# The down product of an encoder MLP: operands split one step earlier, table work one product earlier, tail scalings reordered

## The chip, the cores and the metric

One core of a Trainium2 chip runs the whole program. The metric is the device time of one execution in microseconds (us); of several runs the median is taken. Lower is better.

## The reference

Two residual layers on a sequence of 1024 tokens with 1024 channels, all in float32. Layer 0 mixes tokens by multi-scale pooling, layer 1 by differential attention with rotary tables. After each mixer comes the same MLP, and the last layer is followed by one RMSNorm:

```python
h = h + mixer(rms_norm(h, mix_norm[i]))
h = h + conv_ffn(rms_norm(h, ffn_norm[i]), ...)     # both layers
return rms_norm(h, final_norm)                      # y * rsqrt(mean(y*y) + eps) * final_norm

def conv_ffn(x, w_up, conv_w, conv_b, w_down):      # D_FF = 2816
    g, u = split(x @ w_up)
    return (gelu(conv3(g) + conv_b) * u) @ w_down   # the last product is the "down" product
```

The attention of layer 1 needs cos and sin of positions times inverse frequencies (the rotary tables) and a number lambda from four 64-element vectors.

## The kernel before, in words

The program runs in stages: pooling, up stage and down stage of layer 0, attention, up stage and down stage of layer 1. The change lies in the two down stages (function `ffn`, lines 546 to 708) and in the work handed to them: `attention_tables` (885) for layer 0, `final_gain` (1368) and `tail1` (1373) for layer 1.

**Exact products from a fast format.** Each float32 operand is split into a rounded part and a rest: ScalarE copies it into the rounded format (`hi`, line 580), VectorE subtracts (`lo`, line 581). Each product is then three matmuls (hi by hi, hi by lo, lo by hi, line 597).

**The down stage.** A seven-product Strassen scheme is used. The products run in the order `DOWN_ORDER = (1, 2, 6, 7, 4, 5, 3)`. Each has six chunks of the contraction: the first, c = 0, is one block of 256 rows of the weights, the other five are two. A pair of product and chunk is called a step here: steps 0 to 41, six to a product, so that product 1 is steps 0 to 5 and product 3, the last, steps 36 to 41. In every step TensorE goes over four column tiles t = 0 to 3 of the left operand; a step with c = 0 has 12 matmuls, any other 24. Four PSUM banks, one for each t, collect a product. Products 1, 6 and 5 start in fresh banks; the others add on what is there. After a product's last chunk `evict` (609) takes bank t: VectorE adds it to half a row tile of the result (616) and, after the products that finish a half, ScalarE squares that half and sums it (607), for the norm that follows. Product 1's banks are copied by ScalarE (612). Product 2 finishes the first half of tiles 4 to 7, product 4 the first half of tiles 0 to 3, product 5 their second half, product 3 the second half of tiles 4 to 7.

**Operands.** `load_down(s)` (555) loads both operands of step s by two DMAs of up to 512 KB from SyncE's queue (SP), `prep_down(s)` (570) splits them: four instructions, hi and lo of the left operand `m`, hi and lo of the weights `w`; when it ends it issues `load_down(s + 3)`. The split operands lie in the four half-buffers of `hnT` by turns, in steps 36 to 39 in two of them alone (layer 0 fills the other two with the transposed result of tiles 0 to 3 at that time), and in steps 40 and 41 in two buffers `dop` of their own.

**The order is written by hand.** In the down stage the instructions of TensorE, VectorE, ScalarE and SP keep the order in which the code issues them (726). After the matmuls of each t, and after the eviction where there is one, `pump` (651) is called once. It takes the next piece of the first waiting `prep_down`, if that is for a step no more than two ahead of the running one (one ahead for steps 36 to 39), and otherwise a piece of the list `work`. A piece that ends a `prep_down` also lets `pump` go on with the next. `work` gets the last products of the up stage, `add_p1` (622) after product 2, and after product 4 what `extra` gives: the rotary tables and lambda in layer 0, the load of the final norm's weight in layer 1. After product 5 `tails` (628) puts the norm and scaling of tiles 0 to 3 between the matmuls of product 3. In layer 0 that is `norm_to_hnT` (202): ScalarE scales a tile (`xs`, 204), TensorE transposes it (212), the copies are split into `hnT` (131, 132). In layer 1 it is `tail1`: VectorE scales each half by the row's factor and the norm's weight (1377), SP stores it (1378).

**The end of the stage.** Steps 40 and 41 are run together for one t after the other. After each t come its eviction, the row factor `rstd` (180: add, ScalarE's square root, four more small VectorE instructions) and at once the scaling of that tile. In layer 0 the transposes of a tile follow two tiles later.

**Around it.** Outside these stretches a scheduler places the instructions; in the attention stage only TensorE's order is written out. Weights of the attention are loaded and split in gaps of layer 0's down stage.

Of the kernel before, what the change touches and what calls it, by code (L numbers as in the profile page):

```python
# [20 lines left out]
P = 128  # L21
# [68 lines left out]
def trunk_kernel(  # L90
# [47 lines left out]
    def row_bcast(ap):  # L138
        return ap.partition_broadcast(P)
# [223 lines left out]
    def ffn(layer, ar, tail, extra=None):  # L363
# [205 lines left out]

        def prep_down(s):  # L570
            n = CHUNKS[steps[s][1]][1]
            k = s % 4 if s < last else 2 + s % 2
            if s < len(steps) - 2:
                hi, lo = (t[:, 4 * (k % 2):4 * (k % 2) + 4] for t in hnT[k // 2])
            else:
                hi, lo = ar.dop[s % 2]
            ops = []
            for x, o in zip(stage.pop(s), (0, 2)):
                h_, l_ = hi[:, o:o + n], lo[:, o:o + n]
                A.copy(h_, x)  # L580
                V.tensor_tensor(l_, x, f32(h_), ALU.subtract)  # L581
                ops += [h_, l_]
                yield
            dops[s] = ops
            if s > 1:
                load_down(s + 3)
# [60 lines left out]
        def down_all():  # L647
# [2 lines left out]

            def pump(k=1):
                for _ in range(k):
                    if queue and queue[0][0] <= now[0] + (1 if last <= queue[0][0] < len(steps) - 2 else 2):
                        if next(queue[0][1], "end") == "end":
                            queue.pop(0)
                            pump()
                    elif work:
                        if next(work[0], "end") == "end":
                            work.pop(0)
# [8 lines left out]
            for s, (i, c) in enumerate(steps[:-2]):  # L668
                now[0] = s
                while s not in dops:  # L670
                    pump()
                if s < NT:
                    tt = (s + 4) % NT
                    nc.sync.dma_start(ar.h[tt], h_dram[3 * layer][tt])
                fresh = i in (1, 6, 5) and c == 0
                for t in range(4):
                    if fresh:
                        banks[t] = ar.tile("ps_up", [P, 512], F32, "dn")
                    mms(s, t, fresh, c == nc_ - 1)
                    if c == nc_ - 1:  # L680
                        evict(i, t)
                    pump()
                    next(after, None)
                if c == nc_ - 1:
                    if i == 2:
                        work.append(add_p1())
                    elif i == 4 and extra is not None:
                        work.append(extra())
                    elif i == 5:
                        after = tails()  # L690
# [5 lines left out]
            for t in range(4):  # L696
                for s in (len(steps) - 2, len(steps) - 1):
                    mms(s, t, False, s == len(steps) - 1)
                evict(3, t)
                tl = tail(t + 4, rstd(sq[1][:, t:t + 1]))  # L700
                next(tl, None)
                ends.append(tl)
                if t > 1:
                    for _ in ends[t - 2]:
                        pass
            for tl in ends[2:]:
                for _ in tl:
                    pass

        load(0)  # L710
        first = prep(0)
# [12 lines left out]
                load(j + 2)  # L724
        ar.open_down()
        with tc.manual_schedule(engines=ENGINES | {mybir.EngineType.SP}):
            down_all()


    xr = x.rearrange("b (t p) d -> (b t) p d", p=P)  # L730
# [154 lines left out]
    def attention_tables():  # L885
# [7 lines left out]
        posi = w[:, 816:816 + NT].bitcast(positions.dtype)  # L893
        nc.sync.dma_start(inv, cst[:, C_INV:C_INV + 32])
        nc.sync.dma_start(posi, positions.rearrange("(t p) -> p t", p=P), allow_slow_non_contiguous=True)
        V.tensor_copy(posf, posi)
        yield
        for t in range(NT):
# [18 lines left out]
        A.activation(sinT, nn, AF.Sin)  # L917
        A.activation(cosT, nh, AF.Sin)
        yield
        l = ar.tile("gc", [P, D], F32, "lam")  # L920
        lv = l[:, 0:256].rearrange("p (i f) -> p i f", f=64)
        lp = l[:, 256:384].rearrange("p (i f) -> p i f", f=64)
        ls, le = l[:, 384:386], l[:, 386:388]
        for i, src in enumerate((lam_q1, lam_k1, lam_q2, lam_k2)):
            nc.sync.dma_start(lv[:, i], row_bcast(src[0]))
        V.tensor_tensor(lp, lv[:, 0:4:2], lv[:, 1:4:2], ALU.mult)
        V.tensor_reduce(ls, lp, AX.X, ALU.add)
        A.activation(le, ls, AF.Exp)
        V.tensor_tensor(neglam, le[:, 1:2], le[:, 0:1], ALU.subtract)
        V.tensor_scalar(neglam, neglam, -LAM_INIT, None, ALU.add)  # L930
        nc.sync.dma_start(subsc, subln[0].rearrange("(e o) -> e o", o=1))
        V.tensor_scalar(subsc, subsc, 1.0 - LAM_INIT, None, ALU.mult)


# [433 lines left out]
    def final_gain():  # L1368
        fin.append(ar.tile("gc", [P, D], F32, "gf"))
        nc.sync.dma_start(fin[0], row_bcast(final_norm))  # L1370
        yield

    def tail1(tt, r):
        y, gf = ar.h[tt], fin[0]
        for n in range(2):
            hs = halves(y)[n]
            V.scalar_tensor_tensor(hs, hs, r, halves(gf)[n], ALU.mult, ALU.mult)
            nc.sync.dma_start(halves(outr[tt])[n], hs)
            if n == 0 and tt < 4:
                yield  # L1380
        return
        yield

    for _ in mlp:
# [28 lines left out]
```

## Time and profile before

| | |
|---|---|
| median of 3 runs | 2119.53 us (2117.35 to 2125.2) |
| the profiled execution, its own time | 2117.11 us |
| its span, first to last instruction | 2115.3 us |
| TensorE matmul busy | 2015.5 us, 95% of the span |
| VectorE / ScalarE / GpSimd busy | 1558.6 / 1020.1 / 899.8 us |
| mean granted TensorE clock | 0.98 of full speed |
| down stage of layer 0, of layer 1 | 528 to 760 us, 1886 to 2115.3 us |

Times of rows are microseconds from the start of the span; durations in the timeline are us. PE is TensorE, PEld its weight load, DVE VectorE, ACT ScalarE, POOL GpSimd, SP SyncE. A busy PE is not PE at its peak, since its matmuls are pipelined: the distance from one matmul's start to the next says more than the busy share. In the timeline a bracket gives the idle time of the engine just before the instruction and what ended it. PEclk is the granted TensorE clock as a share of full speed.

### The profile page before, as it was taken

Reading aid. Unit: us, or ns where it says so; the run is one execution under the profiler, and the core shown is the slowest. Engines: PE = TensorE matmul, PEld = TensorE weight load, DVE = VectorE, ACT = ScalarE, POOL = GpSimd, SP = SyncE. Lnnn points to the kernel's source line nnn. Section 1 sums busy time; section 2 is a strip of 40 time slices with the busy share of each in tenths; the row PEclk is TensorE's granted clock in tenths of the full one; section 3 lists DMA queues with packets and bytes.
Section 4 is the critical chain, followed back from the end, with each engine's and each line's share of the span. In section 5 each row is a group of like instructions: output and inputs, shape, how many; then the busy total and the mean of one; then the engine's idle time right before and its main releaser. Section 6 shows DMA issues by size and latency. Waiting matters only on the chain.

```text
span 2115.3 us, 27608 instructions
## 1 busy us (share of the span) xinstructions
PE 2015.5 (95%) x9659; PEld 1669.5 (79%) x9659; DVE 1558.6 (74%) x2278; ACT 1020.1 (48%) x1830; POOL 899.8 (43%) x689
## 2 busy tenths in 40 slices
PE   6789999999999799999999998987999999999997
PEld 5678888888888677888888887876888888888885
DVE  7867777777584648899889987767667777774646
ACT  7643333333453545676667666555433333344433
POOL 4599999995000000101110111024999999920000
PEclk8899999999999999999999999998999999999999
DMA  4225454554965412122212216253346445467653
GB/s 168 95 84 181 138 190 138 158 177 144 375 211 174 163 54 67 48 72 62 61 46 73 57 40 224 90 189 110 120 144 198 146 161 167 139 227 278 205 201 130
DMA packets 221720, 301.90 MB, mean 143 GB/s; under 512 B 17852, under 2 KB 142092, under 8 KB 218764
## 3 DMA queue, kind: packets, MB, share of 16 engines
q1 hardware_dynamic: 221580, 300.13, 43.4%
q8 instruction: 76, 1.25, 0.2%
q14 instruction: 64, 0.52, 0.1%
HBM read 196.78 MB, written 90.70 MB: 136 GB/s over the span
## 4 chain that ended last, share of the span: by engine, by line
PE 82%; DVE 9%; ACT 3%; DMA 3%; issue 2%; SPq 1%; POOL 0%; DVEq 0%; ACTq 0%; POOLq 0%
PE dn L597 17%; PE up_b L422 16%; PE up_c L422 11%; PE up_a L422 11%; PE pj L1020 6%; PE sc L1106 4%; PE pj L1062 4%; PE po L1148 3%; PE aT L1137 2%; PE pj L1233 2%; DVE nm L1108 1%; PE pp L844 1%; PE pl L824 1%; ACT hnT_hi L580 1%; DVE hnT_lo L581 1%
## 5 line engine op out<-in xcount | busy, mean ns | idle before, releaser
L1088 POOL TENSOR_TENSOR q_lo<-qt,q_hi 128x256 fp32r<-128x256 f32 x64 | 49.7, 777 | 698.3 <-ACT q_hi L1087 616.8
L380 POOL TENSOR_TENSOR w_lo<-s,w_hi 128x512 fp32r<-128x512 f32 x168 | 274.2, 1632 | 17.7 <-ACT w_hi L379 17.2
L597 PE MATMUL dn<-hnT_hi 128*128 128x512 f32 x584 | 229.7, 393 | 12.0 <-ACT hnT_hi L580 11.8
L597 PE MATMUL dn<-hnT_lo,hnT_hi 128*128 128x512 f32 x584 | 230.2, 394 | 4.4 <-DVE hnT_lo L581 4.4
L597 PE MATMUL dn<-hnT_hi,hnT_lo 128*128 128x512 f32 x584 | 228.8, 392 | 0.0
L422 PE MATMUL up_b<-x_hi,w_hi 128*128 128x512 f32 x528 | 207.2, 392 | 5.3 <-ACT x_hi L304 4.4
L422 PE MATMUL up_b<-x_lo,w_hi 128*128 128x512 f32 x528 | 206.6, 391 | 2.3 <-DVE x_lo L305 2.3
L380 POOL TENSOR_TENSOR w_lo<-raw,w_hi 128x512 fp32r<-128x512 f32 x130 | 195.3, 1503 | 30.6 <-ACT w_hi L379 26.4
L422 PE MATMUL up_b<-x_hi,w_lo 128*128 128x512 f32 x528 | 206.2, 391 | 0.0
L379 ACT CAST w_hi<-s 128x512 fp32r<-128x512 f32 x176 | 108.4, 616 | 178.9 <-PE up_b L422 87.4
L1108 DVE TENSOR_REDUCE nm<-sc 128x1 f32<-128x1024 f32 x128 | 155.7, 1216 | 15.4 <-PE sc L1106 14.6
L1111 ACT ACTIVATE prob<-sc,nm 128x1024 f32<-128x1024 f32 x128 | 142.7, 1115 | 22.3 <-DVE nm L1108 11.7
L422 PE MATMUL up_a<-hnT_hi,w_hi 128*128 128x512 f32 x352 | 139.3, 396 | 1.4 <-ACT g L499 0.9
L597 PEld LDWEIGHTS dn<-hnT_hi 128*128 128x128 f32 x584 | 110.5, 189 | 37.1 <-ACT hnT_hi L580 13.5
L422 PE MATMUL up_a<-hnT_lo,w_hi 128*128 128x512 f32 x352 | 138.9, 395 | 0.1
L422 PE MATMUL up_a<-hnT_hi,w_lo 128*128 128x512 f32 x352 | 138.5, 394 | 0.0
L394 POOL TENSOR_TENSOR s<-raw 128x512 f32<-128x512 f32 x84 | 133.1, 1584 | 10.3 <-DMA raw<-in_ffn_w_up_dram 4.1
L422 PE MATMUL up_c<-hnT_hi,w_lo 128*128 128x512 f32 x352 | 137.0, 389 | 0.2 <-DVE w_lo L380 0.2
L422 PE MATMUL up_c<-hnT_hi,w_hi 128*128 128x512 f32 x352 | 136.9, 389 | 0.0
L422 PE MATMUL up_c<-hnT_lo,w_hi 128*128 128x512 f32 x352 | 136.9, 389 | 0.0
L581 DVE TENSOR_TENSOR hnT_lo<-mst,hnT_hi 128x1024 fp32r<-128x1024 f32 (+1 forms) x80 | 90.2, 1127 | 61.3 <-ACT hnT_hi L580 61.1
L597 PEld LDWEIGHTS dn<-hnT_lo,hnT_hi 128*128 128x128 f32 x584 | 110.5, 189 | 31.0 <-DVE hnT_lo L581 8.4
(298 smaller groups left out, 5362.6 us busy)
## 6 DMA issues: line engine op xcount, KB each, us to landing
raw<-in_ffn_w_up_dram SPq DMA_DIRECT2D x88, 512.0 KB, 4.3
mst<-m_dram SPq DMA_DIRECT2D x70, 512.0 KB, 5.8
wd<-in_ffn_w_down_dram SPq DMA_DIRECT2D x22, 1024.0 KB, 6.0
wd_dram<-wd SPq DMA_DIRECT2D x22, 1024.0 KB, 6.4
m_dram<-cm SPq DMA_DIRECT2D x80, 256.0 KB, 5.6
wst<-wd_dram SPq DMA_DIRECT2D x40, 512.0 KB, 4.8
m_dram<-gc SPq DMA_DIRECT2D x66, 256.0 KB, 6.3
wst<-in_ffn_w_down_dram SPq DMA_DIRECT2D x30, 512.0 KB, 6.1
```

What stands on the lines that cost most here:

```text
L379: A.copy(hi, src)
L380: eng.tensor_tensor(lo, src, f32(hi), ALU.subtract)
L394: eng.tensor_tensor(t, a, b, op)
L422: PE.matmul(acc, l[a][:, k], r[b][:, k], start=first and n == 0, stop=n == 11, skip_group_check=True)
L581: V.tensor_tensor(l_, x, f32(h_), ALU.subtract)
L597: PE.matmul(banks[t], l[:, q, cols], r[:, q], start=first and cnt == 0, stop=stop and cnt == 3 * n - 1, skip_group_check=True)
L1020: PE.matmul(acc, l[:, k % 2, h], r[:, k], start=(n == 0), stop=(n == 3 * NK - 1))
L1062: PE.matmul(acc, l[:, k % 4], r[:, k], start=(n == 0), stop=(n == 3 * NK - 1))
L1106: PE.matmul(sc[:, ns_], l[:, c], ks[:, c, ns_], start=(l is qhi), stop=(l is qlo))
L1108: V.tensor_reduce(nm, sc, AX.X, ALU.max, negate=True)
L1111: A.activation(soft[j, i][c], sc, AF.Exp, bias=nm, accum_out=sm[:, c, i:i + 1])
L1148: PE.matmul(po, l[:, k], r[:, k], start=(n == 0), stop=(n == 3 * NT - 1))
```

## The change

Nothing of what is computed changes, and the number of matmuls stays. In `ffn`:

```diff
         def prep_down(s):
             n = CHUNKS[steps[s][1]][1]
-            k = s % 4 if s < last else 2 + s % 2
-            if s < len(steps) - 2:
-                hi, lo = (t[:, 4 * (k % 2):4 * (k % 2) + 4] for t in hnT[k // 2])
+            if s < last or s in (last + 2, last + 3):
+                hi, lo = (t[:, 4 * (s % 2):4 * (s % 2) + 4] for t in hnT[s % 4 // 2])
             else:
                 hi, lo = ar.dop[s % 2]
...
-                    if queue and queue[0][0] <= now[0] + (1 if last <= queue[0][0] < len(steps) - 2 else 2):
+                    if queue and queue[0][0] <= now[0] + 3:
...
-                    elif i == 4 and extra is not None:
+                    elif i == 7 and extra is not None:
                         work.append(extra())
...
                 evict(3, t)
-                tl = tail(t + 4, rstd(sq[1][:, t:t + 1]))
-                next(tl, None)
-                ends.append(tl)
+                if t:
+                    next(ends[t - 1], None)
+                ends.append(tail(t + 4, rstd(sq[1][:, t:t + 1])))
                 if t > 1:
                     for _ in ends[t - 2]:
                         pass
-            for tl in ends[2:]:
-                for _ in tl:
-                    pass
+            next(ends[3], None)
+            return ends[2:]
...
         with tc.manual_schedule(engines=ENGINES | {mybir.EngineType.SP}):
-            down_all()
+            ends = down_all()
+        for tl in ends:
+            for _ in tl:
+                pass
```

Steps 36, 37, 40 and 41 now use the two `dop` buffers, steps 38 and 39 the second `hnT` pair. In the last part the scaling of a tile is issued after the eviction of the next one and ahead of that one's `rstd`; what is left of the last two tiles (in layer 0 their transposes, copies and stores) comes after the stretch with the order written by hand.

In `attention_tables` the loads of the four lambda vectors and of `subsc` are issued with those of the frequencies and positions, and four empty pieces follow before the first instruction that uses them:

```diff
+        for i, src in enumerate((lam_q1, lam_k1, lam_q2, lam_k2)):
+            nc.sync.dma_start(lv[:, i], row_bcast(src[0]))
+        nc.sync.dma_start(subsc, subln[0].rearrange("(e o) -> e o", o=1))
+        for _ in range(4):
+            yield
         V.tensor_copy(posf, posi)
...
-        for i, src in enumerate((lam_q1, lam_k1, lam_q2, lam_k2)):
-            nc.sync.dma_start(lv[:, i], row_bcast(src[0]))
         V.tensor_tensor(lp, lv[:, 0:4:2], lv[:, 1:4:2], ALU.mult)
...
-        nc.sync.dma_start(subsc, subln[0].rearrange("(e o) -> e o", o=1))
```

For layer 1's end, the final norm's weight is multiplied into the finished first halves of tiles 4 to 7 as pieces of `work`; the last scaling of such a half is then ScalarE's, and the second half comes first:

```diff
         nc.sync.dma_start(fin[0], row_bcast(final_norm))
-        yield
+        for _ in range(8):
+            yield
+        for tt in range(4, NT):
+            hs = halves(ar.h[tt])[0]
+            V.tensor_tensor(hs, hs, halves(fin[0])[0], ALU.mult)
+            yield
 
     def tail1(tt, r):
         y, gf = ar.h[tt], fin[0]
-        for n in range(2):
+        for n in (1, 0):
             hs = halves(y)[n]
-            V.scalar_tensor_tensor(hs, hs, r, halves(gf)[n], ALU.mult, ALU.mult)
+            if n == 0 and tt >= 4:
+                A.mul(hs, hs, r)
+            else:
+                V.scalar_tensor_tensor(hs, hs, r, halves(gf)[n], ALU.mult, ALU.mult)
             nc.sync.dma_start(halves(outr[tt])[n], hs)
-            if n == 0 and tt < 4:
+            if n and tt < 4:
                 yield
-        return
         yield
```

## Rows read from the trace of the kernel before

**Rows 1.** Busy time by stretch: us, engines (instructions), PEclk, DMA share, GB/s

```profile
528.00:760.00 232.00, 219.42 (x965) 178.66 (x963) 139.77 (x217) 110.35 (x158) 0.00 (x0) 0.98 0.64 218
760.00:1440.00 680.00, 659.15 (x3573) 549.14 (x3574) 564.45 (x1084) 424.32 (x922) 96.51 (x176) 0.99 0.29 86
```

**Rows 2.** Chain of waits in both down stages: start, us, what

```profile
528.17 57.13 PE dn L597 x252
...
591.30 83.34 PE dn L597 x365
...
729.94 0.96 PE tp L212 x8
...
1886.34 57.13 PE dn L597 x252
```

**Rows 3.** Instructions of tile dn: min/median/max ns, first and last start us

```profile
L597 PE MATMUL dn<-dopa_hi,dopa_lo x16: 388/389/397, 747.5 to 758.6; 128*128 128x512 f32 x16
...
L597 PE MATMUL dn<-dopb_hi,dopb_lo x16: 388/389/389, 2093.3 to 2103.5; 128*128 128x512 f32 x16
```

**Rows 4.** Timeline of TensorE in layer 1's step from product 5 to 3

```profile
2066.73 0.39 PE L597 MATMUL dn<-hnT_hi,hnT_lo 128*128 128x512 f32 x1
...
2068.40 0.50 PE L597 MATMUL dn<-hnT_lo,hnT_hi 128*128 128x512 f32 x1 [0.22 <-DVE hnT_lo L581]
...
2070.80 0.39 PE L597 MATMUL dn<-hnT_hi,hnT_lo 128*128 128x512 f32 x1
...
2075.17 0.79 PE L597 MATMUL dn<-hnT_lo,hnT_hi 128*128 128x512 f32 x1 [0.77 <-DVE hnT_lo L581]
```

**Rows 5.** Busy time by stretch, layer 1 from product 5 to 3

```profile
2066.00:2079.00 13.00, 8.73 (x29) 5.98 (x29) 9.49 (x17) 7.92 (x13) 0.00 (x0) 0.87 0.42 136
```

**Rows 6.** Timeline of TensorE in layer 0, products 5 and 3

```profile
692.74 0.39 PE L597 MATMUL dn<-hnT_hi 128*128 128x512 f32 x1
694.67 0.50 PE L597 MATMUL dn<-hnT_lo,hnT_hi 128*128 128x512 f32 x1 [1.55 <-DVE hnT_lo L581]
...
715.31 0.39 PE L597 MATMUL dn<-hnT_hi,hnT_lo 128*128 128x512 f32 x1
...
729.31 0.63 PE L597 MATMUL dn<-hnT_hi,hnT_lo 128*128 128x512 f32 x1
```

**Rows 7.** Timeline of VectorE in layer 0, the two waits for loads

```profile
692.15 0.17 DVE L896 CAST tbl<-tbl 128x8 f32<-128x8 int32 x1 [4.98 <-DMA tbl<-in_positions_dram]
...
719.12 0.29 DVE L926 TENSOR_TENSOR lam<-lam 128x128 f32<-128x128 f32 x1 [4.43 <-DMA lam<-in_diff_lam_k_dram]
```

**Rows 8.** Timeline of VectorE, layer 0, evictions of product 2 (step 11)

```profile
584.04 0.69 DVE L616 TENSOR_TENSOR hda<-dn,hda 128x512 f32<-128x512 f32 x1 [10.99 <-PE dn L597]
...
590.02 1.23 DVE L581 TENSOR_TENSOR hnT_lo<-wst,hnT_hi 128x1024 fp32r<-128x1024 f32 x1 [1.73 <-ACT hnT_hi L580]
591.16 1.28 DVE L616 TENSOR_TENSOR hda<-dn,hda 128x512 f32<-128x512 f32 x2
```

**Rows 9.** Timeline of ScalarE, layer 0, the square behind the first of them

```profile
584.76 0.60 ACT L607 ACTIVATE dn<-hda 128x512 f32<-128x512 f32 x1 [12.44 <-DVE hda L616]
```

**Rows 10.** Timeline of ScalarE, layer 0, the first tile's scaling in product 3

```profile
719.94 1.03 ACT L580 CAST hnT_hi<-mst 128x1024 fp32r<-128x1024 f32 x1
720.99 1.28 ACT L191 ACT_TABLE_LOAD   x1
722.34 0.30 ACT L191 ACTIVATE rt<-ssd,eps 128x4 f32<-128x4 f32 x1
...
723.52 1.15 ACT L204 ACTIVATE xs<-hda,rs_r 128x1024 f32<-128x1024 f32 x1
```

**Rows 11.** Timeline of VectorE at the end of layer 1

```profile
2099.86 0.68 DVE L616 TENSOR_TENSOR hdb<-dn,hdb 128x512 f32<-128x512 f32 x1
...
2103.97 0.68 DVE L616 TENSOR_TENSOR hdb<-dn,hdb 128x512 f32<-128x512 f32 x1
...
2110.84 1.41 DVE L1377 SCALAR_TENSOR_TENSOR hdb<-hdb,rs_r,gf 128x512 f32<-128x512 f32 x2
```

More of the change, by code (lines that the diff above doesn't have):

```diff
@@ L895, in attention_tables @@
         nc.sync.dma_start(posi, positions.rearrange("(t p) -> p t", p=P), allow_slow_non_contiguous=True)
+        l = ar.tile("gc", [P, D], F32, "lam")
+        lv = l[:, 0:256].rearrange("p (i f) -> p i f", f=64)
+        lp = l[:, 256:384].rearrange("p (i f) -> p i f", f=64)
+        ls, le = l[:, 384:386], l[:, 386:388]
+        for i, src in enumerate((lam_q1, lam_k1, lam_q2, lam_k2)):
[3 more added lines that the diff above has]
+            yield
         V.tensor_copy(posf, posi)
@@ L919, in attention_tables @@
         yield
[L920 to L923, printed above, removed]
-        for i, src in enumerate((lam_q1, lam_k1, lam_q2, lam_k2)):
-            nc.sync.dma_start(lv[:, i], row_bcast(src[0]))
         V.tensor_tensor(lp, lv[:, 0:4:2], lv[:, 1:4:2], ALU.mult)
```

## The prediction, on record before the change was run

> **What bounds the kernel now.** I read the busy times by stretch first. In both down stages TensorE is the busy engine, VectorE has 139.8 us of work in 232 and ScalarE 110.4 [rows 1], so the question is where TensorE waits. Then the chain of waits: it runs over TensorE, and its first piece has 252 matmuls in 57.13 us [rows 2], 0.2267 us from start to start, with no wait. A down stage has 4 x (12 + 24 x 5) / 4 x 7 = 924 matmuls, so it can't take less than 209.5 us. Layer 0's began at 528.2 and its last matmul at 758.6 [rows 2, 3], 230.6 us with that matmul; five groups of transposes lie between, at up to 0.96 each [rows 2], 4.8. So 16.3 us are lost; call it 16.5, since later groups run a little faster. Layer 1's began at 1886.3, its last matmul at 2103.5 [rows 2, 3]: 217.4, lost 7.9.
>
> Where they are lost the timeline of TensorE shows. Layer 1, from product 5 to 3 (I call this the seam): 2066.73 to 2068.40 is 1.67 for two matmuls, 1.2 lost; 2070.80 to 2075.17 is 4.37 for two, 3.9 lost, both on a split [rows 4]; and the granted clock over these 13 us is 0.87 [rows 5], the lower of its two levels (1.2 against 2.4 GHz) for some (1 - 0.87) x 13 / 0.5 = 3.4 us, about 1.7 more. Together 6.8 of 7.9; the other 1.1 are short waits of the same kind elsewhere. Layer 0 has the same seam, but worse: 715.31 to 729.31 is 14.0 us for 12 matmuls (2.7), 11.3 lost, and another 1.7 at 692.74 [rows 6]. VectorE shows why: it stood 4.43 us on the lambda vectors and 4.98 us on the positions, loaded just ahead of their use [rows 7], and the splits were queued behind.
>
> After layer 1's last matmul at 2103.5 the program still runs to 2115.3 through VectorE: one tile's eviction, factor and two scalings take 4.11 us (2099.86 to 2103.97) [rows 11], while TensorE delivers a tile each 12 x 0.2267 = 2.72.
>
> **Lead of three steps.** Nothing is added; the same four split instructions of a step are issued one step (5.44 us, at c = 0 2.72) earlier. The buffers stay four deep before step 36, so a split still can't begin until the step four before it is finished. What changes is its place in the queues against the evictions, which wait for TensorE: VectorE stood 10.99 us idle ahead of one [rows 8], with the next splits behind it. Now one more step's operands lie ahead of that point. The short waits go (1.1 in layer 1, where fresh banks follow an eviction with squares): splits late by half a microsecond get 5.44 us.
>
> The seam keeps a wait, a different one. In step 35 the evictions now alternate with the splits of step 38, which are full size (in steps 36 and before: half size). The same alternation stands in step 11: eviction t = 0 begins at 584.04, ScalarE's square (0.60) and the splits (1.03 on ScalarE, 1.23 on VectorE) follow in turn, and the evictions of t = 2 and 3 run from 591.16 to 592.44 [rows 8 to 10]. So t = 2 is evicted about 7.8 us after t = 0 began. Product 3 adds on the same banks, so step 36 may write bank 2 only then. TensorE gets there 18 + 6 matmuls after t = 0, at 5.4. Wait: 2.4 in each layer. Bounds: 0 (VectorE and ScalarE caught up) and 6.8, the seam of today.
>
> In layer 0 the first transposes come after half of step 37: TensorE is there at 7.8 + 0.7 + 0.7 + 2.7 = 11.9. ScalarE starts the split of step 39 after its last square, at 8.4 + 0.8 = 9.2; from such a split's start to the end of the first tile's scaling takes 723.52 + 1.15 - 719.94 = 4.7 [rows 10], so 13.9. Wait 2.1; bounds 0 and 4.4 (when the bank's wait is gone). A wait of 1.7 left the matmul behind it at 0.50 and not at 0.63 [rows 6], so I take no clock loss from waits of this size; had it one, 1.7 each as in layer 1 now.
>
> The square root's table load is in that 4.7: it takes 1.28 and the square root starts 0.07 after it [rows 10]. The Trainium skill (ScalarE: Activation LUTs, "What ACT_TABLE_LOAD costs") puts a drain of some 1.38 us beside the load. The trace doesn't show it here; with it the tile would be ready 1.4 later and the whole at 1.4 more.
>
> Sum: layer 0 16.5 - 2.4 - 2.1 = 12.0 gained, layer 1 7.9 - 2.4 = 5.5.
>
> **Tables and loads one product earlier.** This is in layer 0's 12.0. Seven DMAs (two, four, one) leave SP in step 24 in place of steps 30 and 35, behind the loads of step 30; the loads of step 31 come a step later in the queue, so nobody waits for SP. Their use comes after two further steps' splits, some 10 us later, against 5 us that VectorE stood on them [rows 7]. The small VectorE work and two table functions of ScalarE move from product 5 into 4 and 5, where VectorE is 60% busy [rows 1]. The loads of steps 5 and 6 at the stage's start go ahead of the last up-stage products on VectorE; those have until step 5. Cost taken: nothing; if that cover is gone, VectorE's 4.98 again.
>
> **Final weight early.** Four VectorE multiplies of 128x512 in steps 28 to 30; the nearest row is an addition of that size, 0.68 [rows 11], so 2.7 us in all, beside TensorE. They could cost 2.7 if VectorE had no room; it stood 11 us idle ahead of the eviction shown [rows 8], so I take 0. Its load of gf goes from product 5 to product 4, one DMA.
>
> **The end.** The two scalings (1.41, of which 1.33 is not overlapped) leave VectorE's chain of a tile between factor and next eviction. One runs beside the next tile's square. ScalarE's scaling now stands between the square and the square root: it isn't in the trace in this form, between 0.60 (a square of 128x512 [rows 9]) and 1.15 (a scaling twice as wide [rows 10]); I take 0.7, nearest the former, of which 0.3 covers the add that was there. Period 4.11 - 1.33 + 0.4 = 3.2, three times 0.9 earlier: 2.7. After the last factor one scaling follows instead of two: 0.7; the second store still has to be issued behind the first: minus 0.3. Gain 3.1. With 1.15 it is 1.7, at TensorE's pace of 2.72 it is 4.8; if both orders cost the same, 0.
>
> The Trainium skill (same page, "Rules for kernel authors") sends multiplications to VectorE, up to three times faster in bf16. By the rows the two engines are even for float32 (0.71 against 0.60 to 1.15). By the rule, an estimated 2.1 on ScalarE, the period would be 4.6 and the end some 2 us later than now: 2102 in all.
>
> In layer 0's end ScalarE's scaling is 1.15, so per tile only a little is won; the copies of a tile now fill the wait for the last factor. The transposes of two tiles leave the hand order and meet the first projections, which need only tiles 0 to 3 at first. I take 0.5 gained, between -1.2 (one scaling later) and 2.7 (TensorE's idle stretch there).
>
> **Sum.** 12.0 + 5.5 + 3.1 + 0.5 = 21.1. The profiled execution took 2117.1: 2096.0. The median of the runs is 2.4 above it, 2098.4. I forecast 2097.
>
> **Rivals.** *Lead on paper only.* With four buffers before and after, ScalarE and VectorE may be as far ahead as they can be already, and the seams stay. Then only the waits on loads go: 1.7 at 692.74, and 11.3 less the 5.5 of layer 1's same stretch; with the ends, 1.7 + 5.8 + 3.1 + 0.5 = 11.1: 2107. For it: the 10.99 us of idle time. Against: that idle time stands behind an eviction in the queue, and the late splits stand behind it too.
>
> *Nothing is left.* The evictions of step 35 are not held by the splits and both new waits vanish: 16.5 + 7.9 + 3.6 = 28.0: 2090. For: 365 matmuls in 83.34 us [rows 2], 0.228 each, run over the seams 6 to 7 and 7 to 4, where banks are kept, splits are full size and nothing is squared. Against: the squares here.
>
> *Slower by re-planning.* In the attention stage only TensorE's order is written; the other engines' orders come from the scheduler, and two tiles of layer 0 and the start of the tables now reach it otherwise. It is 680 us long [rows 1] and has 64 blocks. From 21.1 / 64 = 0.33 us a block the gain is eaten; at 0.5 the whole takes 2128. For: VectorE is busy 564 of 680, so order matters there. Against: none of its inputs or waits changes, its weights are loaded in the down stage's gaps as before.
>
> **Chances.** Forecast 0.67 (2092 to 2103 with its bounds), lead on paper 0.18, nothing left 0.08, re-planning 0.07. A change under 0.5% (10.6 us) can't be told from none here; half of the second case lies inside that, so faster 0.84, same 0.10, slower 0.06. The range takes in the first three cases, 2089 to 2108.
>
> **What would show it.** Right: no idle time on the lambda and position loads; matmuls of steps 13 and 31 at 0.227; one wait of 2 to 3 us at each seam, ended by an eviction and not by a split; in layer 0 a second, ended by the scaling of tile 0; the granted clock 1.00 over layer 1's seam; evictions at the end 3.2 us apart. Wrong: a split still ends the seam's wait, the clock still falls there, or the attention stage gets longer than 680 us.

## The result, and the profile after

| us | before | after |
|---|---|---|
| median of the timed runs | 2121.94 (2117.35 to 2125.2, 4 runs) | 2102.02 (2094.27 to 2103.99, 4 runs) |
| the profiled execution, its own time | 2117.11 | 2102.58 |
| its span | 2115.3 | 2100.8 |
| layer 0's down stage, first to last `dn` matmul (start to start) | 230.64 | 218.53 |
| from there to the first projection | 3.95 | 2.46 |
| first projection to layer 1's first `dn` | 1123.58 | 1126.14 |
| layer 1's down stage | 217.30 | 212.05 |
| from its last `dn` matmul to the end of the span | 11.86 | 8.41 |
| layer 0's down stage begins at | 528.0 | 533.2 |

The ratio is 0.99 with an interval of 0.9872 to 0.9928, and in a second comparison (e8 below) 0.9909 (0.9893 to 0.9924). So the changed kernel is faster by about 1%, or some 19 us; 2097 was forecast, with a range of 2089 to 2108. The four stretches in which the two programs differ took 22.3 us less (12.1 + 1.5 + 5.25 + 3.45); the other two rows took 5.2 and 2.6 us more in this execution. Ahead of the down stage every engine has the same instructions in the same order; behind the first projection the order differs in the first 13 us alone, where the last two tiles now come otherwise. These two rows get an experiment of their own.

The chain of waits of the changed kernel (start, us, what) answers to [rows 2]:

```profile
533.38 176.81 PE dn L596 x780
716.78 5.98 PE dn L596 x18
...
1880.50 176.81 PE dn L596 x780
2063.89 20.74 PE dn L596 x90
```

780 matmuls follow one another at 0.2267 us in both layers, with no wait: before, layer 0's first run was cut after 252 and 365. What is left begins after matmul 798, that is at the seam.

The timeline of TensorE of the changed kernel, over the seams of layer 0 and then layer 1, answers to [rows 4, 6]:

```profile
713.87 0.39 PE L596 MATMUL dn<-dopa_hi,dopa_lo 128*128 128x512 f32 x1
716.78 0.50 PE L596 MATMUL dn<-dopa_hi 128*128 128x512 f32 x1 [2.52 <-DVE hda L615]
...
717.34 0.63 PE L596 MATMUL dn<-dopa_hi,dopa_lo 128*128 128x512 f32 x1
...
720.33 0.59 PE L596 MATMUL dn<-dopa_hi 128*128 128x512 f32 x1
720.75 0.39 PE L596 MATMUL dn<-dopa_lo,dopa_hi 128*128 128x512 f32 x1
...
722.79 1.09 PE L212 MATMUL tp<-ident,xs 128*128 128x128 f32 x8
...
2061.01 0.40 PE L596 MATMUL dn<-dopb_hi,dopb_lo 128*128 128x512 f32 x1
2063.89 0.50 PE L596 MATMUL dn<-dopb_hi 128*128 128x512 f32 x1 [2.49 <-DVE hdb L615]
2064.22 0.39 PE L596 MATMUL dn<-dopb_lo,dopb_hi 128*128 128x512 f32 x1
```

Each layer has one wait, 2.52 and 2.49 us of idle time, ended by an eviction (`hda`, `hdb`) and not by a split. Behind layer 0's, eight matmuls stand 0.43 apart (717.34 to 720.75), behind layer 1's 0.23 at once. The transposes at 722.79 have no bracket: they hardly wait.

The busy times by stretch of the changed kernel (us, then PE, PEld, DVE, ACT, POOL busy with instructions, PEclk, DMA share, GB/s): layer 0's down stage, the attention stage, and the two seams; they answer to [rows 1, 5].

```profile
533.00:752.00 219.00, 216.45 (x966) 178.43 (x964) 139.71 (x215) 109.87 (x158) 0.00 (x0) 0.99 0.67 231
754.00:1436.00 682.00, 661.58 (x3574) 550.33 (x3572) 564.43 (x1087) 425.02 (x923) 97.29 (x177) 0.99 0.28 86
711.00:724.00 13.00, 10.45 (x43) 7.94 (x42) 7.91 (x14) 9.13 (x15) 0.00 (x0) 0.87 0.68 242
2058.00:2071.00 13.00, 10.51 (x46) 8.33 (x46) 8.60 (x15) 8.91 (x15) 0.00 (x0) 1.00 0.12 40
```

VectorE's work in the down stage is what it was (139.71 against 139.77): nothing was saved, it only stands elsewhere. The granted clock over layer 1's seam rose from 0.87 to 1.00; over layer 0's it is 0.87, the lower of the two levels (1.2 and 2.4 GHz) for a part of the 13 us.

VectorE of the changed kernel, at the two uses of the table loads, at layer 0's seam and at the end of layer 1, answers to [rows 7, 8, 11]:

```profile
664.39 0.16 DVE L906 CAST tbl<-tbl 128x8 f32<-128x8 int32 x1
...
702.15 0.28 DVE L930 TENSOR_TENSOR lam<-lam 128x128 f32<-128x128 f32 x1
...
708.86 0.69 DVE L615 TENSOR_TENSOR hda<-dn,hda 128x512 f32<-128x512 f32 x1 [0.28 <-PE dn L596]
711.34 1.23 DVE L580 TENSOR_TENSOR hnT_lo<-mst,hnT_hi 128x1024 fp32r<-128x1024 f32 x1 [1.79 <-ACT hnT_hi L579]
712.48 0.68 DVE L615 TENSOR_TENSOR hda<-dn,hda 128x512 f32<-128x512 f32 x1
714.89 1.23 DVE L580 TENSOR_TENSOR hnT_lo<-wst,hnT_hi 128x1024 fp32r<-128x1024 f32 x1 [1.73 <-ACT hnT_hi L579]
716.04 1.28 DVE L615 TENSOR_TENSOR hda<-dn,hda 128x512 f32<-128x512 f32 x2
...
2090.32 0.68 DVE L615 TENSOR_TENSOR hdb<-dn,hdb 128x512 f32<-128x512 f32 x1
...
2093.25 0.69 DVE L615 TENSOR_TENSOR hdb<-dn,hdb 128x512 f32<-128x512 f32 x1
...
2096.30 0.75 DVE L1388 SCALAR_TENSOR_TENSOR hdb<-hdb,rs_r,gf 128x512 f32<-128x512 f32 x1
```

The cast of the positions and the product for lambda have no bracket any more: VectorE no longer stands on these loads. From 708.86 on it goes eviction, square, split on ScalarE, rest on VectorE, eviction: the alternation of [rows 8 to 10] with full-size splits, 3.6 us a turn, so that the eviction of bank 2 begins 7.2 us after that of bank 0. At the end evictions are 2.93 apart, where they were 4.11.

ScalarE of the changed kernel, at the same two places, answers to [rows 10]:

```profile
719.04 1.28 ACT L191 ACT_TABLE_LOAD   x1
720.39 0.30 ACT L191 ACTIVATE rt<-ssd,eps 128x4 f32<-128x4 f32 x1
...
721.58 1.16 ACT L204 ACTIVATE xs<-hda,rs_r 128x1024 f32<-128x1024 f32 x1
...
2094.60 0.70 ACT L1386 ACTIVATE hdb<-hdb,rs_r 128x512 f32<-128x512 f32 x1
```

Tile 0 is scaled by 721.58 + 1.16 = 722.74, 0.05 before TensorE transposes it.

### The profile page after: what moved, and what is told of

It is laid out like the page before. It is cut to its first block, busy times and chain, and to the rows that moved or that the text cites. A ratio compares the mean times of both kernels' runs of the same rounds, so it can differ in the third digit from the quotient of the medians.

```text
span 2100.8 us, 27610 instructions
## 1 busy us (share of the span) xinstructions
PE 2013.0 (96%) x9659; PEld 1670.5 (80%) x9659; DVE 1561.6 (74%) x2278; ACT 1022.1 (49%) x1834; POOL 900.9 (43%) x689
## 3 DMA queue, kind: packets, MB, share of 16 engines
q8 instruction: 76, 1.25, 0.2%
## 4 chain that ended last, share of the span: by engine, by line
PE 83%; DVE 8%; DMA 3%; ACT 3%; issue 2%; SPq 1%; POOL 0%; DVEq 0%; ACTq 0%; POOLq 0%
PE dn L596 19%; PE up_b L422 16%; PE up_c L422 11%; PE up_a L422 11%; PE pj L1023 7%; PE sc L1109 4%; PE pj L1065 4%; PE po L1151 3%; PE aT L1140 2%; PE pj L1236 2%; PE pp L845 1%; PE pl L825 1%; DMA kf<-t 1%; DVE nm L1111 1%; SPq L1044 1%
## 5 line engine op out<-in xcount | busy, mean ns | idle before, releaser
L596 PE MATMUL dn<-hnT_hi 128*128 128x512 f32 x560 | 218.1, 389 | 0.0
L596 PE MATMUL dn<-hnT_hi,hnT_lo 128*128 128x512 f32 x560 | 217.9, 389 | 0.0
L596 PE MATMUL dn<-hnT_lo,hnT_hi 128*128 128x512 f32 x560 | 217.9, 389 | 0.0
L579 ACT CAST hnT_hi<-mst 128x1024 fp32r<-128x1024 f32 (+1 forms) x76 | 74.6, 981 | 131.0 <-PE dn L596 92.1
L394 POOL TENSOR_TENSOR s<-raw 128x512 f32<-128x512 f32 x84 | 133.1, 1585 | 10.3 <-DMA raw<-in_ffn_w_up_dram 4.1
L422 PEld LDWEIGHTS up_b<-x_hi,w_hi 128*128 128x128 f32 x528 | 99.6, 189 | 29.2 <-ACT x_hi L304 5.4
```

Source lines behind the costliest of these rows:

```text
L394: eng.tensor_tensor(t, a, b, op)
L422: PE.matmul(acc, l[a][:, k], r[b][:, k], start=first and n == 0, stop=n == 11, skip_group_check=True)
L596: PE.matmul(banks[t], l[:, q, cols], r[:, q], start=first and cnt == 0, stop=stop and cnt == 3 * n - 1, skip_group_check=True)
```

## The experiments

Three kernels put one part of the change alone into the kernel before, one takes one part out of the kernel after, four go further than it, and four runs repeat known kernels or change the lead. Stage lengths in us; "end" is from the last `dn` matmul to the end of the span. A pitch is the 0.2267 us from one matmul's start to the next, and a wait is what a distance between two starts has above it; a bracket gives idle time alone, which is somewhat less.

| | L0 down | to projection | L1 down | end | ratio to before |
|---|---|---|---|---|---|
| before | 230.64 | 3.95 | 217.30 | 11.86 | |
| e1 lead of three steps alone | 228.95 | 5.63 | 212.03 | 11.86 | 0.9983 (0.9971 to 0.9995) |
| e2 tables earlier alone | 223.67 | 3.95 | 217.29 | 11.86 | 0.9975 (0.9963 to 0.9986) |
| e3 ends alone | 230.48 | 2.47 | 217.35 | 8.41 | 0.9971 (0.9952 to 0.9989) |
| after | 218.53 | 2.46 | 212.05 | 8.41 | 0.99 (0.9872 to 0.9928) |
| e8 after, again | 218.51 | 2.47 | 212.04 | 8.41 | 0.9909 (0.9893 to 0.9924) |
| e7 after, loads late | 218.69 | 2.47 | 212.02 | 8.42 | one run |
| e11 after, lead of two | 221.48 | 2.47 | 215.25 | 9.21 | one run |
| e4 after, no split in step 35 | 215.99 | 2.47 | 209.21 | 8.41 | 0.9895 (0.9879 to 0.9911) |
| e5 e4, scaling ahead of splits | 216.14 | 2.47 | 209.21 | 8.41 | 0.9891 (0.9873 to 0.9909) |
| e6 after, last scaling on VectorE | 218.50 | 2.47 | 212.02 | 8.11 | 0.9913 (0.9899 to 0.9928) |
| e9 joined | 214.64 | 2.47 | 209.21 | 8.11 | 0.9858 (0.9837 to 0.9879) |

**e1, the lead alone.** The kernel before with the new buffers and

```diff
-                    if queue and queue[0][0] <= now[0] + (1 if last <= queue[0][0] < len(steps) - 2 else 2):
+                    if queue and queue[0][0] <= now[0] + 3:
```

> The kernel before with only the buffers and the lead of three steps changed; table loads, their place and the ends as before. Theory (the lead moves splits ahead of the evictions that wait for TensorE): layer 1's down stage, first to last matmul, goes from 217.3 to 212.0 us as in the changed kernel; the wait at the seam from product 5 to 3 is one of 2.7 us, ended by an eviction. Layer 0's goes from 230.6 to 219-222, since the lambda piece now comes some steps later, with more split operands ahead of it, and its 4.4 us on VectorE hit the transposes at most. Ends unchanged: 11.9 us from the last matmul to the end of the span. Time 15 to 17 us below before. Rival (the lead is only on paper, the waits on loads did it): layer 1 stays at 217.3, layer 0 stays above 228, time within 3 us of before.

Layer 1 came as expected, 212.03 with one wait of 2.66. So the lead is worth all of layer 1's 5.25, and it isn't "on paper only". Layer 0 missed: 228.95 where 219 to 222 was expected, and the 1.7 that it gained went again on the way to the first projection (5.63 against 3.95). Why the stage stayed long the timelines of this kernel show, first VectorE, then TensorE:

```profile
729.59 0.29 DVE L925 TENSOR_TENSOR lam<-lam 128x128 f32<-128x128 f32 x1 [5.40 <-DMA lam<-in_diff_lam_k_dram]
```

```profile
725.73 1.09 PE L212 MATMUL tp<-ident,xs 128*128 128x128 f32 x8 [3.39 <-ACT xs L204]
...
735.85 1.16 PE L212 MATMUL tp<-ident,xs 128*128 128x128 f32 x8 [3.30 <-DVE hnT_lo L132]
```

`pump` gives a piece of `work` only where no split is allowed. A longer lead allows more splits first, so the table work slid from step 35 into product 3. The first transposes waited for the scaling of tile 0, ahead of which the two rotary functions with their table load now stood on ScalarE (724.23 + 0.42, the scaling at 724.55). Then VectorE stood 5.40 us on the lambda vectors with the copies of transposed tile 0 behind it, and the transposes of the next tile waited 3.3 for those copies. The wait was not removed but moved to where something else stood behind it.

**e2, the tables alone.** The kernel before with the early loads, the four empty pieces, and

```diff
-                    elif i == 4 and extra is not None:
+                    elif i == 7 and extra is not None:
```

> The kernel before with only the table work one product earlier and its loads issued together and early. Theory: VectorE's waits on positions (4.98 us) and lambda (4.43 us) vanish, the seam in layer 0 becomes that of layer 1 (6.8 us lost): layer 0's down stage 230.6 to 222.5 us, layer 1's stays 217.3; time some 8 us below before. Rival (these waits were covered by the seam's own lateness, only the lead helps): layer 0 stays above 228. Second rival (the earlier table work itself delays the splits of product 4): a new wait of 1 us or more between 650 and 680 us.

The stage fell by 7.0 to 223.67, 1.2 short of the expectation: a split ends a wait of 1.22 in step 32. Table work (683.68 to 685.33) stood there between two evictions, ahead of that split. The same wait of 1.22 at the same matmul is there in e11's layer 0 and gone with a lead of three. In layer 0 the parts alone give 1.7 and 7.0, together 12.1: each covers a loss that the other leaves.

**e3, the ends alone.** The kernel before with the changed order of `rstd` and scalings, `tail1` and `final_gain`.

> The kernel before with only the ends changed: scalings issued after the next tile's eviction, final weight multiplied early into the first halves, ScalarE taking their scaling. Theory: down stages stay 230.6 and 217.3 us from first to last matmul; from layer 1's last matmul to the end of the span 11.9 goes to 8.4 us; from layer 0's last down matmul to the first projection 3.9 goes to 2.5; time 4 to 5 us below before. Rival (the early multiplies cost VectorE time that the seam of layer 1 lacks): layer 1's down stage grows by 1 to 2.8 us and eats half the gain.

8.41 and 2.47, the down stages within 0.2: as expected. The end's gain is its own, and the rival falls: the early multiplies cost layer 1's stage nothing that shows (217.35 against 217.30).

**e7, late loads.** The kernel after with the loads back in front of their uses:

```diff
-        for i, src in enumerate((lam_q1, lam_k1, lam_q2, lam_k2)):
-            nc.sync.dma_start(lv[:, i], row_bcast(src[0]))
-        nc.sync.dma_start(subsc, subln[0].rearrange("(e o) -> e o", o=1))
-        for _ in range(4):
-            yield
         V.tensor_copy(posf, posi)
...
+        for i, src in enumerate((lam_q1, lam_k1, lam_q2, lam_k2)):
+            nc.sync.dma_start(lv[:, i], row_bcast(src[0]))
         V.tensor_tensor(lp, lv[:, 0:4:2], lv[:, 1:4:2], ALU.mult)
```

> The changed kernel with the table loads issued right ahead of their first use again (table work still one product early, lead of three steps kept). Theory (splits stand far enough ahead to cover a wait of 5 us on VectorE): two waits of 4 to 5 us on VectorE are back, but layer 0's down stage stays within 0.5 us of 218.5. Rival (the early loads are needed): layer 0's down stage 221 or more.

VectorE's timeline in this kernel shows both waits of [rows 7] again:

```profile
659.83 0.17 DVE L901 CAST tbl<-tbl 128x8 f32<-128x8 int32 x1 [4.34 <-DMA tbl<-in_positions_dram]
...
697.13 0.29 DVE L928 TENSOR_TENSOR lam<-lam 128x128 f32<-128x128 f32 x1 [4.54 <-DMA lam<-in_diff_lam_k_dram]
```

The stage took 218.69, 0.2 more than after. With splits three steps ahead and the work one product earlier, 4.5 us of idle VectorE cost next to nothing. With this lead, loading early is worth no more than that; what counts is the place of the work: e1, with the same lead and the loads as late, has it one product later and takes 228.95 (the ends, in which the two differ as well, are worth 0.2 there by e3). What early loads are worth with a lead of two no run shows, since e2 has them too.

**e11, a lead of two.** The kernel after with `now[0] + 2`.

> The changed kernel with a lead of two steps for every step, in place of three (before the change it was two, and one for steps 36 to 39). Theory of the prediction (the third step pays: it puts one more step's operands ahead of each eviction in the queues): the short waits of steps 13 and 31 (0.5 and 0.4 us, each ended by a split) come back, the evictions of product 5 now stand in turn with the full-size splits of step 37, so the wait of 2.5 to 2.9 us at the seam stays, and the splits of step 38 come up to 1.5 us late: layer 1's down stage 213 to 215.5 us against 212.05. Rival (all that mattered was the lead of one in steps 36 to 39): 212.0 to 212.3, and no wait on a split anywhere. In layer 0 the same difference, 1 to 3.5 us.

Layer 1 took 215.25, at the upper end of the expectation, but not by all of its reasons. Splits end waits of 0.50 (step 13) and 0.43 (step 31), as expected, and of 0.32 (step 32). No split of step 38 was late. The rest is the clock, as the timelines of VectorE and TensorE in layer 1 show:

```profile
2058.37 0.69 DVE L615 TENSOR_TENSOR hdb<-dn,hdb 128x512 f32<-128x512 f32 x1 [9.83 <-PE dn L596]
2060.79 1.23 DVE L580 TENSOR_TENSOR dopb_lo<-mst,dopb_hi 128x1024 fp32r<-128x1024 f32 x1 [1.73 <-ACT dopb_hi L579]
2061.93 0.69 DVE L615 TENSOR_TENSOR hdb<-dn,hdb 128x512 f32<-128x512 f32 x1
```

```profile
2066.22 0.53 PE L596 MATMUL dn<-dopb_hi 128*128 128x512 f32 x1 [2.45 <-DVE hdb L615]
...
2067.41 0.63 PE L596 MATMUL dn<-dopb_hi 128*128 128x512 f32 x1
```

The alternation is the same with step 37's splits (`dopb`), and so is the idle time, 2.45; but here eight matmuls run 0.43 apart behind it, 1.6 us more. So of the 3.2 us between a lead of two and of three some 1.25 are waits on splits, 0.3 the slower matmul behind each of them, and 1.6 the clock. The end's 0.8 lies behind the last scaling, in the last stores, and its cause stays open: the evictions are 2.93 apart here too.

**e4, no split between product 5's evictions.** The kernel after with

```diff
-                    pump()
+                    if not (i == 5 and c == nc_ - 1):
+                        pump()
```

> The changed kernel with one thing more: no piece of a split is issued in step 35, between the evictions of product 5; step 38's splits follow the last eviction. Theory (the wait of 2.7 us that is left at each seam comes from the evictions standing in turn with step 38's splits): the wait of bank 2 goes in both layers; layer 1's down stage 212.05 to about 209.5 us, layer 0's 218.5 to about 215, since the lower clock behind the wait (about 1.8) goes too, if the first transposes don't then wait for tile 0's scaling; if they do, 216 to 217. Rival (the evictions are held by TensorE's own pace or by the squares, not by the splits): the wait stays at 2 us or more in both layers. Second rival (the splits of step 38 are now late): a wait of over 1 us on a split in step 38. Whole program 2.5 to 6 us under the changed kernel.

VectorE at layer 0's seam in this kernel:

```profile
708.48 0.69 DVE L615 TENSOR_TENSOR hda<-dn,hda 128x512 f32<-128x512 f32 x1 [0.26 <-PE dn L596]
709.84 0.69 DVE L615 TENSOR_TENSOR hda<-dn,hda 128x512 f32<-128x512 f32 x1 [0.67 <-PE dn L596]
711.20 0.69 DVE L615 TENSOR_TENSOR hda<-dn,hda 128x512 f32<-128x512 f32 x1 [0.67 <-PE dn L596]
```

The evictions now come 1.36 apart, at TensorE's pace of six matmuls, and wait for it instead of the reverse. Layer 1's stage took 209.21: every wait is gone, 923 pitches are 209.2. In layer 0 the lower clock went with the wait, and the transposes came too soon for the scaling, as TensorE's timeline shows. In the time of the whole program e4 can't be told from e8, which was timed beside it (0.9895 and 0.9909); its gain is read from the stages.

```profile
719.66 1.09 PE L212 MATMUL tp<-ident,xs 128*128 128x128 f32 x8 [1.70 <-ACT xs L204]
```

**e5, the scaling ahead of the splits.** e4, and in product 3 `next(after, None)` stands before `pump()`.

> As the kernel without splits in step 35, and in product 3 each piece of the norm and scaling of tiles 0 to 3 is issued ahead of the piece of a split, not behind it. Theory: ScalarE reaches the scaling of tile 0 one split (1.03 us) or more earlier, so what is left of the first transposes' wait in layer 0 goes: layer 0's down stage 0.5 to 2 us under the kernel without splits in step 35, about 214.5; layer 1's unchanged at about 209.5. Rival (the first transposes don't wait for the scaling any more): no difference in layer 0, or longer, where splits of steps 39 to 41 come too late and a split ends a wait in product 3. Whole program 3 to 7 us under the changed kernel.

216.14: no gain, the rival's figure but not by its reasons: the first transposes still wait, and no split is late. TensorE's timeline:

```profile
718.96 1.10 PE L212 MATMUL tp<-ident,xs 128*128 128x128 f32 x8 [0.71 <-ACT xs L204]
...
725.25 1.16 PE L212 MATMUL tp<-ident,xs 128*128 128x128 f32 x8 [1.08 <-DVE hnT_lo L132]
```

TensorE's idle time ahead of the first tile fell from 1.70 to 0.71, and the second tile's transposes wait 1.08 for the copies of the first.

**e6, the last scaling on VectorE.** The kernel after with

```diff
-                A.mul(hs, hs, r)
+                V.tensor_scalar(hs, hs, r, None, ALU.mult)
```

> The changed kernel with the last scaling of the first half of tiles 4 to 7 on VectorE in place of ScalarE (one multiply of 128x512 by the row's factor); nothing else. Theory (taking that scaling off VectorE's chain of a tile is what made the end shorter): VectorE gets about 0.7 us more per tile, evictions 3.2 to 3.7 apart in place of 2.93, and from layer 1's last matmul to the end 9.0 to 10.5 us in place of 8.41. Rival by the rule that multiplications belong to VectorE: 8.4 or less. Rest of the program unchanged; whole program 0.5 to 2 us over the changed kernel, within what a timing can just tell.

My theory missed and the rival was right: 8.11. VectorE at the end in this kernel:

```profile
2087.39 0.48 DVE L1386 TENSOR_SCALAR hdb<-hdb,rs_r 128x512 f32<-128x512 f32 x1
...
2088.96 0.68 DVE L615 TENSOR_TENSOR hdb<-dn,hdb 128x512 f32<-128x512 f32 x1
...
2091.80 0.69 DVE L615 TENSOR_TENSOR hdb<-dn,hdb 128x512 f32<-128x512 f32 x1
```

The plain multiply takes 0.48 against 0.70 on ScalarE. In both places it stands in the chain of a tile: on VectorE it begins as the square ends and holds back the add, on ScalarE it stood between the square and the square root. From the read-out of the square's sum to the square root it is 0.59 here (2087.38 to 2087.97), 0.70 in the changed kernel (2094.51 to 2095.21) and 0.41 before (2101.11 to 2101.52). Evictions are 2.84 apart in place of 2.93. The timing can't tell 0.3 us.

**e8, after again; e10 and e12, before again.**

> The changed kernel itself, timed beside the others on the same chip. Expected 0.990 of the time before, with an interval of about 0.988 to 0.992; stages as in its first profile: 218.5 and 212.05 us for the two down stages, 8.4 us at the end, and one wait of 2.7 us at each seam, with the lower clock behind it in layer 0 and not in layer 1. If the clock falls in layer 1 this time, or not in layer 0, the difference between the layers is chance and not the place.

> The kernel before once more, for a second profile. The changed kernel's first profile started its up stage 5.2 us later than the kernel before and took 2.6 us longer from the first projection to layer 1's down stage, with the same instructions in the same order there. Theory (both vary from execution to execution, whatever the kernel): here the up stage starts anywhere between 82 and 87.5 us, and the stretch takes 1123 to 1129 us. Rival (the change made them longer): 82.0 and 1123.6 again, both within 0.5. The down stages repeat within 0.3: 230.6 and 217.3 us, end 11.86.

> The kernel before a third time, for one question: the up stage began at 82.0 and 81.6 us in its two profiles, at 87.2 and 82.1 in the changed kernel's, and at 82.1 to 87.1 in the eight others, all of which have the same instructions in the same order before it. Theory (chance of the execution): by the ten others it begins above 83 us in about 8 of 10 executions, so here at 83 to 87.5 more likely than not. Rival (something in the kernel before keeps it at 82): 81.5 to 82.5 a third time, and then some 3 us of the changed kernel's gain are given back at the start on average. Stretch from first projection to layer 1's down stage 1123 to 1129; down stages 230.6 and 217.4.

e8: ratio and stages as expected, and the clock fell in the same layer as in the first profile. The down stages and ends repeat: in e8 within 0.02; in e10 and e12 layer 0's took 230.55 and 230.71, the ends 11.85 and 11.88, layer 1's 217.46 and 218.57, the latter with six more matmuls at the lower clock. The first `dn` piece in the chain of waits of e10, and then of e12:

```profile
527.74 57.13 PE dn L597 x252
```

```profile
533.64 57.13 PE dn L597 x252
```

For the start, e10 alone would have spoken for the rival; e12 refutes it. Before began its down stage at 528.0, 527.6 and 533.5, after at 533.2 and 528.0, and in all five the up stage began some 446 earlier. Over all fourteen profiles it began at 81.6 to 83.3 in five and at 85.7 to 87.5 in nine. From the first projection to layer 1's first `dn` before took 1123.6, 1126.3 and 1121.2, after 1126.1 and 1127.3, the other kernels 1123.2 to 1129.3. So both stretches vary from execution to execution, and the 5.2 and 2.6 us of the first comparison are no effect of the change that could be shown. An effect of a microsecond or two isn't excluded: from the first projection to layer 1's first `dn` the five profiles with the old order of the ends took 1124.7 on average, the nine with the new one 1126.0, and each group spreads over 5 us or more. What sets the start was not looked into.

**e9, joined.** e4 with e6's scaling on VectorE, and the pieces of tiles 0 to 3 one column tile later:

```diff
                 if prev is None:
                     yield
+                    yield
```

> A version meant to beat both: the kernel without splits in step 35, with the last scaling of the first halves on VectorE, and in product 3 the pieces of tiles 0 to 3 behind the first scaling one column tile (1.36 us) later, so that layer 0's first transposes stand where the scaled tile is there. Theory (in the kernel without splits in step 35 the first transposes wait 1.9 us for ScalarE's scaling of tile 0): the wait falls to 0.3 to 0.8, layer 0's down stage 214.4 to 215.0 us against 215.99; layer 1's 209.2 as there; end 8.1. Rival (the transposes of a later tile wait instead, as with the pieces ahead of the splits, where the second tile's waited 1.1): 215.5 or more. Whole program 3.5 to 5 us under the changed kernel, ratio to before about 0.9885.

```profile
714.92 1.09 PE L212 MATMUL tp<-ident,xs 128*128 128x128 f32 x8 [0.34 <-ACT xs L204]
```

That row of its TensorE timeline is what is left of that idle time, 0.34 where it was 1.70; later tiles' transposes don't wait more than in e4. 214.64, 209.21 and 8.11 are 3.9, 2.8 and 0.3 under after, 7.0 together, and the ratio to before is 0.9858 (0.9837 to 0.9879), whose interval lies below that of e8 and overlaps that of the first comparison by 0.0007. By its stages this version beats both; its median is 2089.54 us.

## Why the prediction was right, step by step

| term | forecast | measured |
|---|---|---|
| layer 0's down stage | 12.0 | 12.1 |
| layer 1's down stage | 5.5 | 5.25 |
| end of layer 1 | 3.1 | 3.45 |
| end of layer 0's stage | 0.5 | 1.5 |
| sum | 21.1 | 22.3 |

**Lead.** The short waits went, and the seam's wait changed from splits to an eviction: 2.68 and 2.66, 2.4 forecast. Bank 2 was free 7.9 us after bank 0's eviction began (708.86 to 716.78) where 7.8 was worked out, and TensorE was there at 714.10, after 5.24 (5.4). e4 shows that the alternation is the whole cause. e11 shows what the third step is worth over two, and e1 that a lead alone can make another queue late: "nothing is added" holds for the splits, but not for the pieces of `work`, which move with the lead; the prediction didn't see that.

**Layer 0 was right by luck, by two errors that cancel.** Forecast were 2.4 for the bank, 2.1 for the first transposes, and no loss of clock. Measured are 2.68, about 0.2, and eight matmuls 0.2 us too long, 1.6, with 0.1 at the edge. The tile was ready when it was forecast, 722.74 - 708.86 = 13.9 after bank 0's eviction (13.9); TensorE was late, at 13.7 instead of 11.9, for the lower level had cost it those 1.7 us. The step that failed is "I take no clock loss from waits of this size". Its row was one wait of 1.7; the alternative, 1.7 us each, was named and turns out right in layer 0 and wrong in layer 1. As the scaling was due at 13.9 anyway, the loss cost nothing, and in e4, without it, TensorE came sooner and waited 1.9 for the scaling.

**Tables.** With the lead of three the place of the work was the gain (e1 to e7, both with late loads: 10.3), the early loads were not (e7: 0.2). The prediction had put the 5 us of cover on the loads.

**The end.** The scaling on ScalarE took 0.70 as assumed; the period fell to 2.93 and not 3.2. Half of that is the scaling, which holds back the square root by 0.3 where 0.4 was taken (0.70 against 0.41, as under e6); the other half is the next eviction, which starts 0.08 behind the factor's last instruction, where the scalings had started 0.20 behind it. Three periods give 3 x 1.18 = 3.5, and that is the 3.45: the 0.7 gained behind the last factor was lost again, for from the last scaling's end to the end of the span it is 3.75 now and was 3.05. The prediction's reading that the two engines are even for this multiply was wrong: VectorE's nearest row was a different instruction. The Trainium skill (ScalarE: Activation LUTs, "Rules for kernel authors") was right on the side that it takes, and e6 agrees, though by 0.70 to 0.48 and not by up to three, which it gives for bf16. The drain that the Trainium skill (ScalarE: Activation LUTs, "What ACT_TABLE_LOAD costs") puts beside a table load is not seen after the change either: the square root starts 0.07 us behind the 1.28.

**Layer 0's end.** TensorE's idle time there fell from 2.55 to 1.07, as it waits for the copies of one tile and on ScalarE these no longer stand behind the scaling of the third. 0.5 was taken between bounds of -1.2 and 2.7.

**The rivals.** "Lead on paper only" falls by e1's layer 1. "Nothing is left" falls by the wait that stayed; with e4's edit it would have been nearly right for layer 1. "Slower by re-planning" falls by e10 and e12, as a loss that would eat the gain: 1121 to 1126 before, 1126 to 1127 after. The time came out 5 us above the forecast with 22.3 gained in place of 21.1, and both intervals (15 to 27 us, and 16 to 23) hold 22.3; the start, which varies by 5 us, is large enough for the rest, but that it was the start isn't shown.

## What to carry to other kernels

In queues that keep their order, ask of every instruction that waits what stands behind it: a lead moves splits out from behind an eviction, but whatever takes their place in the turn is held by the same alternation, and leaving the queue empty between evictions was worth another 2.5 us in layer 0 and 2.8 in layer 1 here. Work given out "where there is room" moves when the priorities in front of it change, so try a lead and the place of such work together: alone they gave layer 0's stage 1.7 and 7.0, together 12.1. Before a wait is costed, work out when its next waiter's other operand is ready; a delay that ends before that time is free, and removing it gains nothing.

## What was not expected of the hardware

- The same idle time of TensorE had two outcomes. After 2.52 us in layer 0 the granted clock fell to the lower level for some 3.4 us; after 2.49 us in layer 1 it stayed at 1.00, in both profiles of this kernel and in e1, e6 and e7. With a lead of two it fell in layer 1 as well, after 2.45. So neither the layer nor the length of the wait decides by itself; what does stays open.
- On VectorE a multiply of 128x512 float32 by one factor a row took 0.48 us, the same with a second tensor as operand 0.74, an addition of two tensors 0.68.
